# A hybrid retention and attention block on Trainium2: another table of times for side work in the attention, and stores issued by another engine

## The chip, the cores and the metric

The kernel runs on one core of one Trainium2 chip. The metric is the device time of one execution in microseconds; a profile shows one execution, engine by engine. TensorE (PE) multiplies matrices, VectorE (DVE), ScalarE (ACT) and GpSimd (POOL) do elementwise work, and SyncE (SP) issues nearly all DMA transfers. Each engine runs its own list of instructions strictly in order and waits at an instruction until its inputs are there; a DMA transfer is issued by an instruction of some engine's list and then runs on the DMA engines.

## The reference

One layer in fp32, for a sequence of 1024 tokens of width 1024, with 16 learned meta tokens put in front:

```python
u = _rms_norm(h, pre_w)
z = u @ w_in                       # one input projection for all branches
rq, rk, rv, rg, aq, ak, av, ag, gr, ga = _split_in(z)
...                                # bidirectional retention, 4 heads -> o_r, normed, gated by silu(rg)
y_r = o_r.astype(h.dtype) @ w_rb
...
o_a = _windowed_sink_attention(aq, ak, av, sink)[:, META_PAD:].reshape(B, T, ATT_Q)
o_a = o_a * jax.nn.silu(ag.astype(jnp.float32))
y_a = o_a.astype(h.dtype) @ w_ab
mix = jax.nn.sigmoid(gr) * y_r + jax.nn.sigmoid(ga) * y_a
out = mix @ w_o
return h + _rms_norm(out, post_w)
```

The attention has 8 heads of 128 in 2 key groups, a window of 128 positions to either side, the meta tokens always visible, and a sink logit per head; `aq` and `ak` are rotated by position first.

## The kernel before

Every fp32 matrix is split into a high and a low part, and `mm3` (L74 to L76) does three matmuls for one product. The program goes through setup and first projections, the retention heads (to about 335 us), the attention (to about 565 us), and then four phases of large products: gates (z), the retention branch, the attention branch and the output projection. The large products use a scheme with seven block products instead of eight, which needs sums and differences of blocks of the operands. Those of x are made on the side during the attention, and go to DRAM (`xs_d`); some blocks of the gates' product are worked out in the attention too (`pe`), and go to DRAM as `e`.

The attention is 32 chunks (hp, n): a pair of heads hp = 0 to 3, a block of 128 queries n = 0 to 7; the text writes chunk k = 8 hp + n. Chunk k of the loop issues stage 1 of chunk k + 1 (scores `ps` on PE, mask and maximum `raw`, `nm` on VectorE at L1369, exp `p` on ScalarE at L1372, scaling by 1/sum on POOL, in the last two chunks on ScalarE at L1379), stage 2 of chunk k (transposes `pt` on PE, high parts `pah`, `pm`, `pbh` on ScalarE, low parts on VectorE), 5 to 10 steps of filler for PE, and stage 3 of chunk k - 1 (output products `po`, copied by ScalarE to `oa`, L1440, and stored to `oTa_d` after each second chunk, L1443).

A step of filler is one `mm3`: 200 steps in all, of projections of later queries and keys (`paq`, `pak`) and of the partial gate products `pe7` to `pe13`. A projection's result is rotated by `rope_late`: two products on VectorE (`m_aq`, `aq`), and two transfers by POOL that add `m_aq` into `aq` (`akr` and `m_ak` for keys). `split_q` then makes the high and low half of queries (`aqh` by ScalarE at L641, `aql` by VectorE), `keys` those of keys (`kTh` by ScalarE at L687, `kTl` by VectorE).

Side work is hung on the steps by the table `BEGUN`: after step number s, `hooked` issues the functions of entry s. They are
- `sum_fetch`, `sum_row`: load row q of 8 of x (two tiles `xs0q`, `xs1q` of 256 KB each, two buffers), scale it on ScalarE (L726), four differences on VectorE (L729), store it by SP (L732);
- `fetch_aq`, `fetch_ak`, `half_w`: load weights (`wr`, two buffers) and split them (`wh` by ScalarE at L116, `wl` by VectorE). `wr17` holds those of the last queries;
- `pre_fetch`, `pre_sum`, `pre_parts`: load the weights of one partial gate product (`we`, 512 KB each, in the same two buffers), three sums on VectorE (L774), high part `weh` on ScalarE (L784), low part `wel` on VectorE. After the last one the buffers go to the first weights of z (`wrz`).

The scheduler that turns the program into one list for each engine keeps the order of the text where `issue_after` says so; else it moves instructions by its own costs. Three 1 MB pieces of x are copied from DRAM to DRAM into the output by `x_to_out` on SP's queue (the normed result is added to them at the end). The copy waits for nothing; `issue_after` only fixes its place, behind the last store of `oTa`:

```python
            if k in (12, 17, 21):
                x_to_out({12: 0, 17: 4, 21: 6}[k])
```

The stores of `e` (20, L806) and of `oTa` (16, L1443) are issued by SP, in one list with all loads.

Of the kernel before, what the change touches and what calls it, by code (L numbers as in the profile page):

```python
# [16 lines left out]
P = 128  # L17
# [21 lines left out]
def block_kernel(ctx: ExitStack, tc: tile.TileContext, x0, xT, x, meta, w_in, w_rb, w_ab, w_out, post_w,  # L39
                 rope, tab, out):  # L40
    nc = tc.nc
# [17 lines left out]
    oTa_d = dram.tile([KT, P, SEQ], F32, tag="oTa", name="oTa_d")  # L59
# [5 lines left out]
    e_d = {(u, p): dram.tile([P, 512], F32, tag=f"e{u}{p}", name=f"e{u}_{p}") for u in PRE for p in PRE[u]}  # L65
    xs_d = [dram.tile([4, P, 2, 512], F32, tag=f"xs{i}", name=f"xs{i}") for i in range(2)]
# [120 lines left out]
    def rope_evac(t, a, b, o, nm):  # L187
# [13 lines left out]
    neg, na, e, e2, s_, ss, acc, lg = (ra.tile([P, 8], F32, name=n) for n in (  # L201
        "neg", "na", "e", "e2", "s_", "ss", "acc", "lg"))
# [63 lines left out]
    with tc.tile_pool(name="setup", bufs=1, reuse_waits="tile") as st:  # L266
# [57 lines left out]
        for k in range(KT):  # L324
            t = xr[k]
# [395 lines left out]
    def sum_row(q, part):  # L721

        k, c = q // 2, slice(256 * (q % 2), 256 * (q % 2) + 256)
        if not part:
            for i, t in xsum.items():
                nc.scalar.activation(t, t, AF.Copy, scale=vec[:, 4 * i + k:4 * i + k + 1])  # L726
# [31 lines left out]
    def pre_fetch(u):  # L758
        n = P * len(PRE[u])
        raw = [keep.tile([P, 4, 256], F32, tag="wr", bufs=2, name=f"we{u}_{j}") for j in range(len(PRE[u]))]  # L760
        for j, t in enumerate(reversed(raw)):
            nc.sync.dma_start(t[:, :, 0:n], w_in[gates[u], :, 4 - 4 * j:8 - 4 * j, 0:n])
        fetched_w[u] = raw

    def pre_sums(u, only=range(3)):

        raw, n = fetched_w[u], P * len(PRE[u])
        t = raw[-1]
        if n > P:
            v = t[:, :, P:n]  # L770
            for i in only:
                a, b, op = ((raw[0][:, :, P:n], v, ALU.add), (v, raw[0][:, :, 0:P], ALU.subtract),
                            (t[:, :, 0:P], v, ALU.subtract))[i]
                nc.vector.tensor_tensor(v, a, b, op)  # L774
# [4 lines left out]
    def pre_parts(u):  # L779

        t, n = fetched_w.pop(u)[-1], P * len(PRE[u])
        h = wp.tile([P, 4, 256], R, tag="wh", bufs=4, name=f"weh{u}")[:, :, 0:n]
        l = wp.tile([P, 4, 256], R, tag="wl", bufs=4, name=f"wel{u}")[:, :, 0:n]
        nc.scalar.copy(h, t[:, :, 0:n])  # L784
        dve_lo(l, t[:, :, 0:n], h)
        parts[u] = h, l

    def gen_pre(u):

        if u not in parts:  # L790
            if u not in fetched_w:
                pre_fetch(u)
                pre_sums(u)
            pre_parts(u)
        h, l = parts.pop(u)
        for p in PRE[u]:
# [8 lines left out]
            nc.scalar.copy(o, b)  # L805
            nc.sync.dma_start(e_d[u, p], o)  # L806
            yield

    def hooked(gens, at):
# [522 lines left out]
    def attention():  # L1332
        oa = [None]
# [95 lines left out]
        def stage3(hp, n):  # L1429
            g = hp // 2  # L1430
            bl, m = st2.pop((hp, n))
            po = p3(f"po{hp}_{n}")
            for j, (b, h_, l_) in enumerate(bl):
                mm3(po[:, 0:256], *(t[:, P * g:P * g + P] for t in (vah[:, b], low_value(b))), h_, l_, j == 0, False)
            latest[:] = [nc.tensor.matmul(po[:, 0:256], vm[:, P * g:P * g + P], m, start=False,
                                          stop=True).ins]
            if n % 2 == 0:
                oa[0] = ap.tile([P, 2, 256], F32, tag="oa", bufs=2, name=f"oa{hp}_{n}")
            o0 = P * (n % 2)
            last["oa"] = nc.scalar.copy(oa[0][:, :, o0:o0 + P],  # L1440
                                        po[:, 0:256].rearrange("p (e t) -> p e t", e=2)).ins
            if n % 2:
                stored.append(nc.sync.dma_start(  # L1443
                    oTa_d[2 * hp:2 * hp + 2, :, P * (n - 1):P * (n + 1)].rearrange("e p t -> p e t"), oa[0]).ins)

# [12 lines left out]
        for k, (hp, n) in enumerate(chunks):  # L1458
            ends = k >= len(chunks) - 2
            if k + 1 < len(chunks):  # L1460
                with follow(*latest, *marks("oa", "lo")):
                    stage1(*chunks[k + 1])
                if chunks[k + 1] == (1, NB - 1):
                    keys(1, 0)
            if chunks[k] == (3, NB - 2):

                with follow(*latest):
                    fill(FILL[hp][n])
                yield
            if not k:  # L1470
                with follow(*latest):
                    fill(FILL[hp][n] - 3)
            with follow(*latest, *marks("exp", "sum")) if not ends else ExitStack():
                stage2(hp, n)
            if k and not ends:
                with follow(*latest):
                    fill(FILL[hp][n])
            with follow(*latest) if not ends else ExitStack():
                if k:
                    stage3(*chunks[k - 1])  # L1480
            if ends:
                yield
            if k in (12, 17, 21):
                x_to_out({12: 0, 17: 4, 21: 6}[k])
        stage3(*chunks[-1])


# [9 lines left out]
             82: [(split_q, 2, 0, 0)], 88: [(sum_row, 3, 0)], 89: [(sum_row, 3, 1)], 90: [(split_q, 2, 1, 0)],  # L1497
             91: [(sum_fetch, 4)], 96: [(sum_row, 4, 0)], 97: [(sum_row, 4, 1)], 99: [(sum_fetch, 5)],
             104: [(keys, 1, 1)], 105: [(fetch_aq, 3)], 107: [(sum_row, 5, 0)], 108: [(sum_row, 5, 1)],
             110: [(sum_fetch, 6)], 112: [(split_q, 2, 0, 1)], 114: [(half_w, 'q', 3, 0)],  # L1500
             116: [(half_w, 'q', 3, 1)], 118: [(pre_fetch, 9)], 121: [(sum_row, 6, 0)], 122: [(sum_row, 6, 1)],
             123: [(keys, 1, 2)], 124: [(sum_fetch, 7)], 125: [(pre_sum, 9, 0)], 128: [(pre_sum, 9, 1)],
             129: [(split_q, 2, 1, 1)], 130: [(pre_sum, 9, 2)], 133: [(pre_parts, 9)], 134: [(pre_fetch, 10)],
             136: [(keys, 1, 3)], 139: [(sum_row, 7, 0)], 140: [(sum_row, 7, 1)], 145: [(split_q, 3, 0, 0)],
             146: [(pre_sum, 10, 0)], 147: [(pre_sum, 10, 1)], 149: [(pre_sum, 10, 2)], 152: [(split_q, 3, 1, 0)],
             153: [(pre_parts, 10)], 154: [(pre_fetch, 11)], 161: [(pre_sum, 11, 0)], 162: [(pre_sum, 11, 1)],
             163: [(pre_sum, 11, 2)], 164: [(split_q, 3, 0, 1)], 167: [(pre_parts, 11)], 168: [(pre_fetch, 12)],
             169: [(split_q, 3, 1, 1)], 173: [(pre_sum, 12, 0)], 174: [(pre_sum, 12, 1)], 175: [(pre_sum, 12, 2)],
             177: [(pre_parts, 12)], 178: [(pre_fetch, 13)], 182: [(pre_sum, 13, 0)], 183: [(pre_sum, 13, 1)],
             184: [(pre_sum, 13, 2)], 187: [(pre_parts, 13)]}  # L1510

    def x_to_out(r):

        with tc.issue_after(stored[-1]):
            nc.sync.dma_start(out[P * r:P * r + 2 * P], x[P * r:P * r + 2 * P])

    del wak[:]
    i = attention()
    next(i)

# [102 lines left out]
```

## Time and profile before

| | |
|---|---|
| median of 3 runs | 1069.37 us (1068.57 to 1070.4) |
| profiled execution | 1068.98 us |
| its span on the core | 1067.2 us |
| granted TensorE clock over the span | 0.995 |
| busy PE / VectorE / ScalarE / POOL | 1050.3 / 839.7 / 505.8 / 233.0 us |

The span runs from the first to the last instruction of the profile; the profiled execution's own time is 1.8 us longer. A row of the timeline gives start, duration, engine, line and operation, what is written and read, and in brackets how long the engine was idle before it and what ended the wait. SPq and POOLq are the engines' issues of DMA. Windows give, for each stretch, its length and then the busy time of PE, of its weight loads, and of the other engines, the granted clock of TensorE and the mean busy share of the DMA engines. Names in rows of the profile have no buffer numbers: `we` there stands for `we9_1` as well as for `we10_1`.

### The profile page before, as it was taken

What the parts mean: (1) busy time and instruction counts of PE and PEld (TensorE: products, weight loads), DVE (VectorE), ACT (ScalarE), POOL (GpSimd) and SP (SyncE); (2) the same over time, 40 slices, a digit from 0 to 9 for tenths busy, and PEclk for the clock granted to TensorE, in tenths of its full rate; (3) what the DMA queues carried; (4) which work ended last, traced back from release to release, by engine and by line L of the source; (5) the groups of instructions that cost most, each with busy time, mean ns of one, the idle gap of its engine ahead of it and who ended that gap; (6) DMA issues with size and microseconds to landing.
All of it is one profiled execution on the core that took longest, in us unless ns stands there. A gap on an engine that the chain in (4) does not pass through costs nothing.

```text
span 1067.2 us, 17268 instructions
## 1 busy us (share of the span) xinstructions
PE 1050.3 (98%) x5880; PEld 908.4 (85%) x5880; DVE 839.7 (79%) x1788; ACT 505.8 (47%) x1127; POOL 233.0 (22%) x338
## 2 busy tenths in 40 slices
PE   9999999999999999989999999999999999999997
PEld 8998999989999888977888888887888888788886
DVE  7886768758875777767768988998799799778665
ACT  5531422523424566555667544455456546334433
POOL 3345245243342432524310000000000000011032
PEclk9999999999999999989999999999999999999999
DMA  9433222242331465665548769899934756789463
GB/s 351 165 84 85 79 32 80 70 109 75 103 72 50 110 187 159 161 203 143 149 154 285 246 228 332 272 348 353 372 117 158 242 172 227 223 222 321 122 119 79
DMA packets 96760, 188.44 MB, mean 177 GB/s; under 512 B 10945, under 2 KB 35553, under 8 KB 95857
## 3 DMA queue, kind: packets, MB, share of 16 engines
q1 hardware_dynamic: 86352, 172.33, 48.0%
q0 software_dynamic: 10176, 14.73, 9.2%
q8 instruction: 46, 0.75, 0.3%
q10 hardware_dynamic: 144, 0.29, 0.1%
q14 instruction: 42, 0.34, 0.1%
HBM read 124.32 MB, written 57.68 MB: 171 GB/s over the span
## 4 chain that ended last, share of the span: by engine, by line
PE 89%; DMA 5%; DVE 3%; ACT 1%; issue 1%; DVEq 0%; POOLq 0%; POOL 0%; ACTq 0%; SPq 0%
PE bz L75 7%; PE bz L74 7%; PE bz L76 7%; PE pv L76 3%; PE pv L75 3%; PE pv L74 3%; PE ba L75 2%; PE br L74 2%; PE br L75 2%; PE ba L74 2%; PE ba L76 2%; PE br L76 2%; PE bo L75 2%; PE bo L74 2%; PE bo L76 2%; PE paq L75 2%
## 5 line engine op out<-in xcount | busy, mean ns | idle before, releaser
L1246 POOL DMA_DIRECT2D mx_d<-c1a x4 | 3.6, 890 | 402.4 <-DVE c1a L1237 383.2
L75 PE MATMUL bz<-T,llz 128*128 128x512 f32 x192 | 76.2, 397 | 0.0
L74 PE MATMUL bz<-T,lhz 128*128 128x512 f32 x192 | 75.6, 395 | 0.0
L76 PE MATMUL bz<-T,lhz 128*128 128x512 f32 x192 | 75.4, 393 | 0.0
L74 PE MATMUL pv<-wh,big 128*128 128x256 f32 x256 | 73.4, 287 | 0.0
L75 PE MATMUL pv<-wh,big 128*128 128x256 f32 x256 | 73.2, 286 | 0.0
L76 PE MATMUL pv<-wl,big 128*128 128x256 f32 x256 | 73.2, 286 | 0.0
L75 PE MATMUL bz<-big,llz 128*128 128x512 f32 x176 | 69.6, 395 | 0.2 <-DVE llz L90 0.2
L76 PE MATMUL bz<-big,lhz 128*128 128x512 f32 x176 | 69.5, 395 | 0.0
L74 PE MATMUL bz<-big,lhz 128*128 128x512 f32 x176 | 68.8, 395 | 0.2 <-ACT lhz L942 0.2
L1382 POOL TENSOR_SCALAR p<-p,den 128x400 f32<-128x400 f32 (+1 forms) x60 | 40.4, 776 | 80.6 <-DVE den L1375 73.8
L1372 ACT ACTIVATE p<-raw,nm 128x401 f32<-128x401 f32 (+1 forms) x64 | 38.2, 599 | 41.1 <-DVE nm L1369 40.9
L74 PE MATMUL paq<-big,wh 128*128 128x512 f32 x128 | 51.8, 404 | 0.0
L75 PE MATMUL paq<-big,wl 128*128 128x512 f32 x128 | 50.6, 395 | 0.0
L76 PE MATMUL paq<-big,wh 128*128 128x512 f32 x128 | 50.6, 395 | 0.0
L76 PEld LDWEIGHTS pv<-wl,big 128*128 128x128 f32 x256 | 48.3, 189 | 0.4
L74 PEld LDWEIGHTS pv<-wh,big 128*128 128x128 f32 x256 | 48.3, 188 | 0.4
L75 PEld LDWEIGHTS pv<-wh,big 128*128 128x128 f32 x256 | 48.3, 189 | 0.3
L1369 DVE CUSTOM_DVE_ANT_0 raw<-ps,mask,nsink 128x400 f32<-128x400 f32 (+1 forms) x64 | 36.3, 598 | 10.7 <-PE ps L76 10.2
L90 DVE TENSOR_TENSOR wl<-wr,wh 128x1024 fp32r<-128x1024 f32 x28 | 34.9, 1250 | 11.8 <-POOL wh L87 6.8
L74 PEld LDWEIGHTS bz<-T,lhz 128*128 128x128 f32 x192 | 36.0, 188 | 9.1 <-ACT u2z L1024 0.2
L76 PEld LDWEIGHTS bz<-T,lhz 128*128 128x128 f32 x192 | 36.0, 188 | 8.8
(616 smaller groups left out, 3613.1 us busy)
## 6 DMA issues: line engine op xcount, KB each, us to landing
wrz<-in_w_in_dram SPq DMA_DIRECT2D x32, 512.0 KB, 5.7
wr<-in_w_in_dram SPq DMA_DIRECT2D x29, 512.0 KB, 3.7
e<-e SPq DMA_DIRECT2D x40, 256.0 KB, 4.2
we<-in_w_in_dram SPq DMA_DIRECT2D x16, 512.0 KB, 4.3
tg<-tg_d SPq DMA_DIRECT2D x32, 256.0 KB, 4.7
T<-preT SPq DMA_DIRECT2D x6, 1024.0 KB, 7.9
xn<-in_x_dram SPq DMA_DIRECT2D x8, 512.0 KB, 9.2
oTr_d<-ost SPq DMA_DIRECT2D x16, 256.0 KB, 2.1
```

The source lines that it names most:

```text
L74: nc.tensor.matmul(o, ah, bh, start=first, stop=False, **kw)
L75: nc.tensor.matmul(o, al, bh, start=False, stop=False, **kw)
L76: latest[:] = [nc.tensor.matmul(o, ah, bl, start=False, stop=last, **kw).ins]
L90: return nc.vector.tensor_tensor(o, i, hi.bitcast(F32), ALU.subtract).ins
L1246: nc.gpsimd.dma_start(d, to, accum_op=ALU.add)
L1369: nc.vector.tensor_tensor_reduce(raw[e_][:, 1:1 + wid], s[:, 0:wid], mask[:, mo:mo + wid], -SCALE, nsink[:, hd:hd + 1], ALU.add, ALU.min, ...
L1372: last["exp"] = nc.scalar.activation(p[:, 0:1 + wid], raw[e_][:, 0:1 + wid], AF.Exp, scale=-1.0, bias=nm_[:, e_:e_ + 1], accum_out=den[:, ...
L1382: nc.gpsimd.tensor_scalar(pt[e_][:, 0:wid], pt[e_][:, 0:wid], den[:, e_:e_ + 1], 1.0, op0=ALU.mult, op1=ALU.mult)
```

## The change

It does three things. The table `BEGUN` gets other steps. Rows 0 to 7 of x are summed at 34, 48, 61, 75, 88, 100, 123 and 146 (before: 34, 48, 74, 88, 96, 107, 121 and 139) and loaded at 10, 39, 52, 65, 79, 92, 105 and 127 (before: 10, 39, 52, 78, 91, 99, 110 and 124). Loads, first sums and halves of the partial gate products 9 to 13 go to 122, 141, 158, 171, 182 (before 118, 134, 154, 168, 178), to 133, 150, 166, 176, 187 (before 125, 146, 161, 173, 182) and to 140, 157, 170, 181, 190 (before 133, 153, 167, 177, 187). The halves of the last queries' weights go to 117 and 121 (before 114 and 116), keys (1, 2) to 116 (before 123), and some `split_q` and `fetch_aq` move by two to eight steps. Second, the copies of x follow chunks 12, 14 and 21, each behind the latest store of a row of sums. Third, ScalarE issues the stores of `e` and `oTa`. The line numbers of the changed kernel are one lower than before from the table on.

```diff
--- before.py
+++ after.py
@@ -729,7 +729,7 @@
             nc.vector.tensor_tensor(x[o], x[a], x[b], ALU.subtract)
         if part:
             for i, t in xsum.items():
-                nc.sync.dma_start(xs_d[i][k][:, :, c], t)
+                last["xs"] = nc.sync.dma_start(xs_d[i][k][:, :, c], t).ins
 
     xsum = {}
 
@@ -803,7 +803,7 @@
                     yield
             o = ra.tile([P, 512], F32, tag="m", bufs=4, name=f"e{u}_{p}")
             nc.scalar.copy(o, b)
-            nc.sync.dma_start(e_d[u, p], o)
+            nc.scalar.dma_start(e_d[u, p], o)
             yield
 
     def hooked(gens, at):
@@ -827,7 +827,7 @@
             yield from gen_pre(u)
 
     pre, fetched_w, parts = all_pre(), {}, {}
-    softmax, stored, last = [], [], {}
+    softmax, last = [], {}
 
     def marks(*names):
         return [last[m] for m in names if m in last]
@@ -1440,8 +1440,8 @@
             last["oa"] = nc.scalar.copy(oa[0][:, :, o0:o0 + P],
                                         po[:, 0:256].rearrange("p (e t) -> p e t", e=2)).ins
             if n % 2:
-                stored.append(nc.sync.dma_start(
-                    oTa_d[2 * hp:2 * hp + 2, :, P * (n - 1):P * (n + 1)].rearrange("e p t -> p e t"), oa[0]).ins)
+                nc.scalar.dma_start(
+                    oTa_d[2 * hp:2 * hp + 2, :, P * (n - 1):P * (n + 1)].rearrange("e p t -> p e t"), oa[0])
 
 
 
@@ -1480,8 +1480,8 @@
                     stage3(*chunks[k - 1])
             if ends:
                 yield
-            if k in (12, 17, 21):
-                x_to_out({12: 0, 17: 4, 21: 6}[k])
+            if k in (12, 14, 21):
+                x_to_out({12: 0, 14: 4, 21: 6}[k])
         stage3(*chunks[-1])
 
 
@@ -1492,26 +1492,25 @@
...
-             61: [(split_q, 1, 0, 1)], 65: [(split_q, 1, 1, 1)], 68: [(half_w, 'k', 1, 0)],
-             72: [(half_w, 'k', 1, 1)], 74: [(sum_row, 2, 0)], 75: [(sum_row, 2, 1)], 78: [(sum_fetch, 3)],
...
+             61: [(sum_row, 2, 0)], 62: [(sum_row, 2, 1)], 65: [(sum_fetch, 3)], 66: [(split_q, 1, 0, 1)],
...
     def x_to_out(r):
 
-        with tc.issue_after(stored[-1]):
+        with tc.issue_after(last["xs"]):
             nc.sync.dma_start(out[P * r:P * r + 2 * P], x[P * r:P * r + 2 * P])
 
     del wak[:]
```

The first place is ScalarE's list around the key cast `kTh1_2` (hp 2, chunks 17 and 18; in the names, `p2_2` is the exp of chunk (2, 2), `wh17_0` and `wh17_1` are the halves of the last queries' weights, `xs06` and `xs16` the tiles of row 6). Before:

```order
L116 CAST wh17_0_6420<-wr17_0_6266 128x1024
L116 CAST wh17_1_6430<-wr17_1_6267 128x1024
L1440 COPY oa1_6_6380<-po1_7_6457 128x2x128
L1372 ACTIVATE p2_2_6469,den2_2_6468<-raw4_6293,nm2_2_6467 128x401
L1372 ACTIVATE p2_2_6469,den2_2_6468<-raw5_6301,nm2_2_6467 128x401
L1410 CAST pah2_1_6496<-pt1_2_1_6487 128x512
L1413 CAST pm1_4889<-pt2_2_1_6492 32x128 x2
L1420 CAST pbh2_1_6501<-pt2_2_1_6492 128x256
L726 ACTIVATE xs06_6345<-xs06_6345,vec_101 128x512
L726 ACTIVATE xs16_6347<-xs16_6347,vec_101 128x512
L687 CAST kTh1_6206<-akr1_2_6352 128x256
```

Now:

```order
L116 CAST wh17_0_6432<-wr17_0_6256 128x1024
L687 CAST kTh1_6206<-akr1_2_6357 128x256
L1440 COPY oa1_6_6381<-po1_7_6452 128x2x128
L1443 DMA oTa_d_67<-oa1_6_6381 128x2x256
L1372 ACTIVATE p2_2_6464,den2_2_6463<-raw4_6306,nm2_2_6462 128x401
L1372 ACTIVATE p2_2_6464,den2_2_6463<-raw5_6314,nm2_2_6462 128x401
L1410 CAST pah2_1_6491<-pt1_2_1_6482 128x512
L1413 CAST pm1_4889<-pt2_2_1_6487 32x128 x2
L1420 CAST pbh2_1_6496<-pt2_2_1_6487 128x256
L116 CAST wh17_1_6506<-wr17_1_6257 128x1024
```

The key cast stands ahead of the exp instead of behind it, one half of `wh17` has moved behind the next exp, row 6 comes later, and the store of `oa1_6` is an instruction of this list.

The second place is SP's list around the second copy of x (`xs0_91` and `xs1_92` are the DRAM tensors of sums, `out_0_dram` the output). Before:

```order
L762 DMA we9_1_6441<-in_w_in_dram 128x1024
L1443 DMA oTa_d_67<-oa1_6_6380 128x2x256
L1515 DMA out_0_dram<-in_x_dram 16x16384
L762 DMA we9_0_6440<-in_w_in_dram 128x1024
L732 DMA xs0_91<-xs06_6345 256x1x256
L732 DMA xs1_92<-xs16_6347 256x1x256
L719 DMA xs07_6530<-in_xT_dram 128x2x256
L719 DMA xs17_6532<-in_xT_dram 128x2x256
```

Now:

```order
L732 DMA xs0_91<-xs05_6086 256x1x256
L732 DMA xs1_92<-xs15_6088 256x1x256
L1514 DMA out_0_dram<-in_x_dram 16x16384
L719 DMA xs06_6278<-in_xT_dram 128x2x256
L719 DMA xs16_6280<-in_xT_dram 128x2x256
L762 DMA we9_1_6514<-in_w_in_dram 128x1024
L762 DMA we9_0_6513<-in_w_in_dram 128x1024
L732 DMA xs0_91<-xs06_6278 256x1x256
L732 DMA xs1_92<-xs16_6280 256x1x256
```

The copy stands behind the two stores of row 5 and ahead of the loads of row 6, the two loads of `we9` come after it and with nothing between them, and the store of `oa1_6` is gone from the list.

The third place is the end of the attention, where ScalarE's list has the high part of the last partial gate product, `weh13`. Before:

```order
L1420 CAST pbh3_5_7482<-pt2_3_5_7473 128x256
L784 CAST weh13_7495<-we13_1_7343 128x1024
L805 COPY e12_2_7492<-pe12_2_7424 128x512
L1379 ACTIVATE p3_6_7450<-p3_6_7450,den3_6_7449 128x400 x2
L805 COPY e12_3_7512<-pe12_3_7499 128x512
L1440 COPY oa3_4_7526<-po3_4_7515 128x2x128
L1388 COPY pm2_3_6_7466<-p3_6_7450 128x64
```

Now:

```order
L1420 CAST pbh3_5_7479<-pt2_3_5_7470 128x256
L805 COPY e12_2_7489<-pe12_2_7422 128x512
L1379 ACTIVATE p3_6_7447<-p3_6_7447,den3_6_7446 128x400 x2
L806 DMA e12_2_87<-e12_2_7489 128x512
L805 COPY e12_3_7512<-pe12_3_7493 128x512
L1388 COPY pm2_3_6_7463<-p3_6_7447 128x64
L806 DMA e12_3_88<-e12_3_7512 128x512
L1440 COPY oa3_4_7526<-po3_4_7515 128x2x128
L784 CAST weh13_7505<-we13_1_7413 128x1024
```

`weh13` has gone from the first of these to the last, behind the copies of `e12`, the scalings of `p3_6` and two stores.

PE's list at its use: before, `pe13` begins ahead of the transposes of chunk (3, 6):

```order
L76 MATMUL ps7_7_7537<-kTl1_6207,aqh3_11_7191 128x272
L74 MATMUL pe13_2_7548<-big1_0_110,weh13_7495 128x512
L74 MATMUL pe13_3_7564<-big1_0_110,weh13_7495 128x512
L1399 MATMUL pt1_3_6_7625<-ident_118,p3_6_7450 128x128
L1404 MATMUL pt2_3_6_7630<-ident_118,p3_6_7450 128x128
L75 MATMUL pe13_2_7548<-big1_0_110,wel13_7496 128x512
L76 MATMUL pe13_2_7548<-big1_1_112,weh13_7495 128x512
```

Now:

```order
L76 MATMUL po3_5_7646<-pbl3_5_7480,vah_533 128x256
L1435 MATMUL po3_5_7646<-pm1_4889,vm_534 128x256
L74 MATMUL pe13_2_7548<-big1_0_110,weh13_7505 128x512
L74 MATMUL pe13_3_7564<-big1_0_110,weh13_7505 128x512
L75 MATMUL pe13_2_7548<-big1_0_110,wel13_7506 128x512
L76 MATMUL pe13_2_7548<-big1_1_112,weh13_7505 128x512
L74 MATMUL pe13_2_7548<-big1_0_110,weh13_7505 128x512
```

It begins behind those transposes and behind the output products of chunk (3, 5).

More of the change, by code (lines that the diff above doesn't have):

```diff
@@ L1499, in block_kernel @@
[L1499 to L1508, printed above, removed]
@@ L1509, in block_kernel @@
-             177: [(pre_parts, 12)], 178: [(pre_fetch, 13)], 182: [(pre_sum, 13, 0)], 183: [(pre_sum, 13, 1)],
-             184: [(pre_sum, 13, 2)], 187: [(pre_parts, 13)]}
+             61: [(sum_row, 2, 0)], 62: [(sum_row, 2, 1)], 65: [(sum_fetch, 3)], 66: [(split_q, 1, 0, 1)],
+             68: [(half_w, 'k', 1, 0)], 72: [(half_w, 'k', 1, 1)], 73: [(split_q, 1, 1, 1)], 75: [(sum_row, 3, 0)],
+             76: [(sum_row, 3, 1)], 79: [(sum_fetch, 4)], 82: [(split_q, 2, 0, 0)], 88: [(sum_row, 4, 0)],
@@ new lines, in block_kernel @@
+             89: [(sum_row, 4, 1)], 90: [(split_q, 2, 1, 0)], 92: [(sum_fetch, 5)], 100: [(sum_row, 5, 0)],
+             101: [(sum_row, 5, 1)], 102: [(fetch_aq, 3)], 104: [(keys, 1, 1)], 105: [(sum_fetch, 6)],
+             110: [(split_q, 2, 0, 1)], 116: [(keys, 1, 2)], 117: [(half_w, 'q', 3, 0)], 121: [(half_w, 'q', 3, 1)],
+             122: [(pre_fetch, 9)], 123: [(sum_row, 6, 0)], 124: [(sum_row, 6, 1)], 127: [(sum_fetch, 7)],
+             129: [(split_q, 2, 1, 1)], 133: [(pre_sum, 9, 0)], 134: [(pre_sum, 9, 1)], 136: [(keys, 1, 3)],
@@ new lines, in block_kernel @@
+             139: [(pre_sum, 9, 2)], 140: [(pre_parts, 9)], 141: [(pre_fetch, 10)], 145: [(split_q, 3, 0, 0)],
+             146: [(sum_row, 7, 0)], 147: [(sum_row, 7, 1)], 150: [(pre_sum, 10, 0)], 152: [(pre_sum, 10, 1)],
+             153: [(split_q, 3, 1, 0)], 154: [(pre_sum, 10, 2)], 157: [(pre_parts, 10)], 158: [(pre_fetch, 11)],
+             164: [(split_q, 3, 0, 1)], 166: [(pre_sum, 11, 0)], 167: [(pre_sum, 11, 1)], 168: [(pre_sum, 11, 2)],
+             170: [(pre_parts, 11)], 171: [(pre_fetch, 12)], 172: [(split_q, 3, 1, 1)], 176: [(pre_sum, 12, 0)],
@@ L1512, in x_to_out @@
+             178: [(pre_sum, 12, 1)], 179: [(pre_sum, 12, 2)], 181: [(pre_parts, 12)], 182: [(pre_fetch, 13)],
+             187: [(pre_sum, 13, 0)], 188: [(pre_sum, 13, 1)], 189: [(pre_sum, 13, 2)], 190: [(pre_parts, 13)]}
     def x_to_out(r):
-        with tc.issue_after(stored[-1]):
+        with tc.issue_after(last["xs"]):
             nc.sync.dma_start(out[P * r:P * r + 2 * P], x[P * r:P * r + 2 * P])
```

2 lines of the change are left out of this document (removed).

## The prediction

> **What bounds the kernel now.** I read the page first (who is busy, and in which slices not), then the table of windows over the gap that it shows, then PE's waits there, and then what ScalarE, VectorE and the queues did in front of that wait.
>
> ```profile
> span 1067.2 us, 17268 instructions
> PE 1050.3 (98%) x5880; PEld 908.4 (85%) x5880; DVE 839.7 (79%) x1788; ACT 505.8 (47%) x1127; POOL 233.0 (22%) x338
> PE   9999999999999999989999999999999999999997
> PEclk9999999999999999989999999999999999999999
> ```
>
> TensorE is the bound: it is idle for 16.9 us of the whole span. Apart from the tail (the 7 at the end), slice 18 alone (453 to 480 us) falls short, in busy time and in clock. By windows (PE's column comes first; PEclk and the DMA share stand behind the engines):
>
> ```profile
> 460.00:480.00 20.00, 14.96 (x88) 13.59 (x87) 13.32 (x33) 10.17 (x27) 5.27 (x10) 0.83 0.74 226
> 480.00:500.00 20.00, 17.95 (x101) 15.13 (x100) 15.94 (x39) 10.71 (x29) 9.82 (x15) 1.00 0.48 115
> ...
> 470.00:472.00 2.00, 1.05 (x3) 1.04 (x4) 1.86 (x6) 1.17 (x3) 0.02 (x1) 0.50 0.63 212
> 472.00:474.00 2.00, 2.00 (x9) 1.88 (x9) 0.42 (x1) 0.00 (x0) 0.00 (x0) 0.50 0.73 206
> 474.00:476.00 2.00, 2.00 (x11) 1.82 (x10) 0.00 (x0) 0.00 (x0) 0.00 (x0) 0.67 0.97 335
> ```
>
> From 460 to 500 us PE idles 5.04 + 2.05 = 7.1 us. Behind the long gap its clock is 0.50 to 0.67, which costs 1.05 x 0.50 + 2.00 x 0.50 + 2.00 x 0.33 = 2.2 us more. These 9.3 us are the prize; the other 9.8 us of idle time lie outside these 40 us. The waits in this stretch:
>
> ```profile
> PE ps L74 <- ACT kTh L687: 5.0, 1, 5.0
> PE ps L75 <- DVE aql L90: 1.3, 1, 1.3
> PE ps L76 <- DVE kTl L90: 0.4, 1, 0.4
> ```
>
> The scores of chunk (2, 3) wait 5.0 us for the keys kTh1_2. What held ScalarE, and the queues beside it (SP's copy of x at L1515; POOL's transfer of m_aq into aq by L185; rows with DMA behind the time are pieces of the chain; in the last five the number at the end is the median from issue to landing, first of the stretch 463 to 476, then, in the last two, of the whole run):
>
> ```profile
> 454.12 0.62 ACT L641 CAST aqh<-aq 128x512 fp32r<-128x512 f32 x1 [1.83 <-DMA aq<-m_aq]
> 457.38 0.72 ACT L726 ACTIVATE xs<-xs,vec 128x512 f32<-128x512 f32 x1 [2.64 <-DMA xs<-in_xT_dram]
> 461.32 2.00 ACT L116 CAST wh<-wr 128x1024 fp32r<-128x1024 f32 x2
> 469.27 1.33 ACT L726 ACTIVATE xs<-xs,vec 128x512 f32<-128x512 f32 x2
> 470.51 0.39 ACT L687 CAST kTh<-akr 128x256 fp32r<-128x256 f32 x1
> ...
> 461.80 0.82 PE L1399 MATMUL pt<-ident,p 128*128 128x128 f32 x4
> 476.46 0.69 DVE L774 TENSOR_TENSOR we<-we,we 128x512 f32<-128x512 f32 x1 [4.04 <-DMA we<-in_w_in_dram]
> 482.03 0.68 DVE L90 TENSOR_TENSOR aql<-aq,aqh 128x512 fp32r<-128x512 f32 x1
> ...
> 465.99 0.61 SPq L1515 DMA_DIRECT2D out_dram<-in_x_dram  x1
> 438.08 6.08 DMA xs<-in_xT_dram
> 454.56 2.71 DMA xs<-in_xT_dram
> 466.71 9.66 DMA we<-in_w_in_dram
> ...
> we<-in_w_in_dram SPq DMA_DIRECT2D x2, 512.0 KB, 7.4
> aq<-m_aq POOLq DMA_DIRECT2D x2, 128.0 KB, 9.3
> out_dram<-in_x_dram SPq DMA_DIRECT2D x1, 8.7
> ...
> aq<-m_aq POOLq DMA_DIRECT2D x32, 128.0 KB, 3.3
> we<-in_w_in_dram SPq DMA_DIRECT2D x16, 512.0 KB, 4.3
> ```
>
> ScalarE goes through its list in order. It idles 2.64 us for a load of row 5 of the sums, which shifts all behind it (exp, both halves of wh17, 2.00 us); then exp p2_2 must come before the casts of row 6 (1.33 us), and only behind those, at 470.51, kTh1_2. The second stall hangs on the load of we9, issued behind the 1 MB copy of x: 9.66 us. VectorE sits 4.04 us in the first sum of we9, with the masks of the scores queued behind it; aql2_11, late with its rotated queries (9.3 us to landing), comes at 482.03, and PE has waited 1.3 us for it.
>
> **The change part by part.** *Table of rows.* Rows 5 and 6 move from steps 107 and 121 to 100 and 123, and their casts no longer stand between this exp and this key cast. The 2.64 us were the end of a longer string: the store of row 3 was behind the first copy of x, so the load of row 4 took 6.08 us, its sum and store were late, and the load of row 5 was issued only at 454.56. Now a copy is issued behind both stores of a row; the loads of row 5 are issued near 438 and 440, land with the first copy at the latest (438 + 6.1 = 444), and are cast near 447. Rows 6 and 7 are fetched 18 and 19 steps ahead of their sums, against 11 and 15. So this wait goes. One half of wh17 instead of two stands ahead of kTh1_2, and the exp of p2_2 now comes behind it. Worked with the durations above: aqh2_10 ends at 454.74, the exps of p2_1 follow their scores at 456, the cast of half wh17 ends by about 460, and kTh1_2 by 461 (0.39 us). PE's last work ahead of the wait ended at 465.9 (kTh1_2 was done at 470.9, less the 5.0). That leaves 5 us of slack: the 5.04 us go, and with them the 2.2 us of clock.
>
> *we9 and the copy.* The pieces 0, 4 and 6 of x go to DRAM behind the chunks 12, 14 and 21. No copy is then ahead of we9: issued near 467 when wl17_1 frees its buffer, it lands at the median of its kind, 4.3 us, near 472, and its first sum stands 8 steps later than before, at 133 (near 475 without the stall). So the 4.04 us of VectorE go; with its queries not behind a copy, aql2_11 stands ahead of the first we9 sum and is on time. The 1.3 us and what else is in the 2.05 us go too, except for the 0.4 us at kTl, which I keep as a loss: kTl1_3 still stands behind a we9 sum. Gain of the two parts: 9.3 - 0.4 = 8.9 us.
>
> *Stores on ScalarE's queue.* 16 of oTa, 20 of e.
>
> ```profile
> L1443 SPq DMA_DIRECT2D oTa_d<-oa x16: 367/382/879, 362.6 to 577.2; - x16
> L806 SPq DMA_DIRECT2D e<-e x20: 319/326/559, 94.6 to 563.4; - x20
> L288 ACTq DMA_DIRECT2D head<-in_x_dram x1: 402/402/402, 0.7 to 0.7; - x1
> SPq L806 <- ACT e L805: 55.6, 13, 9.7
> ```
>
> The only issue on ScalarE's queue cost 402 ns, SP's 326 to 382 ns. I take 0.40: 36 x 0.40 = 14.4 us of ScalarE, at most one store or three per chunk. ScalarE is busy for 47%, and between its copy of oa and the next exp it waits anyway (0.94 us in the row at 550.77 below), which covers the one oTa store per two chunks. Cover gone, the bound is 14.4 us; I take nothing. On the other side SP no longer stands 55.6 us in waits for e, but what it issues behind them had leads of chunks, so I take no gain either.
>
> *End of attention.* The halves of the partial gate products are made later: the lead of pre_parts ahead of its first use falls from 27, 15, 9, 7 and 5 steps to 20, 11, 6, 3 and 2. The rows there now:
>
> ```profile
> 550.77 0.63 ACT L1372 ACTIVATE p<-raw,nm 128x401 f32<-128x401 f32 x1 [0.94 <-DVE nm L1369]
> 553.30 1.05 ACT L784 CAST weh<-we 128x1024 fp32r<-128x1024 f32 x1
> 557.00 0.52 ACT L1372 ACTIVATE p<-raw,nm 128x273 f32<-128x273 f32 x1 [0.22 <-DVE nm L1369]
> 554.38 1.23 DVE L90 TENSOR_TENSOR wel<-we,weh 128x1024 fp32r<-128x1024 f32 x1
> 556.57 0.64 PE L74 MATMUL pe<-big,weh 128*128 128x512 f32 x2
> 564.66 0.50 PE L75 MATMUL bz<-big,llz 128*128 128x512 f32 x1 [0.15 <-DVE llz L90]
> 555.64 0.33 SPq L1177 DMA_DIRECT2D wrz<-in_w_in_dram  x1
> ```
>
> weh13 stood ahead of the copies of e12, the two scalings of p3_6, pm and oa; all of these ended by 556.8 (557.00 less 0.22). Put behind them, and with two stores (0.8 us) among them, weh13 ends at 557.6 to 557.9 instead of 554.35, and wel13 (1.23) at 559.1 at the latest. PE meets pe13 at 556.57 plus the transposes and the output products that it now does first (about 1.95 us), 558.5; its second product needs wel13 by 559.0. A stall of 0.3 us. wrz0_1, which takes over that buffer, is issued 3.5 us later; the first low half of z then arrives some 0.4 us late, beside 0.15 before. Bounds of the two: nothing, and 3.5 us if the whole delay reaches PE. I take 0.6, since the orders leave PE other work for most of it.
>
> **Sum.** -9.3 + 0.4 + 0.6 = -8.3 us. The profiled execution took 1068.98 us (span 1067.2), which gives 1060.7; the median of the three runs is 0.4 above it, so 1061.1. I forecast **1061**. From no change at all, a measurement of this kernel can tell about 0.2%, 2.1 us.
>
> **Rivals.** *The copy moves the stall.* Behind chunk 14 it is issued near 451.5, between the transfers of aq2_10 and of akr1_2 as they lay before. Before, aq<-m_aq landed 9.3 us after its issue beside a copy, and 3.3 us otherwise. If it is held to the copy's end, 451.5 + 8.7 = 460.2, ScalarE casts aqh2_10 there instead of at 454.12, the exps of p2_1 end near 462, and PE, which takes p2_1 at 461.8, waits 1 to 3 us; with the end of attention at its bound, 3.5, the loss is 1 to 5 us: 1062 to 1066. The Trainium skill, "DMA: Bandwidth & Descriptors", section "Queues, rings and completion order", says that each DMA engine takes turns between the queues at the grain of packets; by that a small transfer from POOL's queue would need about twice its 3.3 us beside the copy, 6.6 us as an estimate, and this stall would not exist. The trace does not bear that out here: 9.3 us, longer than the copy itself. The Trainium skill, "TensorE: Matmul & The Clock Gate", Part 1, puts the fall of the clock at an idle stretch of about 3.4 us; by it only the upper end of this rival would pay in clock too, an estimate of 2.2 us as behind the 5.0 us gap above.
>
> *The stall stays.* The same bytes are moved in the same stage, and the DMA engines are at 0.74 from 460 to 480. If it is this load and not the place of the copy that makes we9 and the rotated rows late, the waits of 4.04 and 2.64 us come back at another load, and the time is 1067.5 to 1070. Against it: the next 20 us have a share of 0.48, so there is room to move into.
>
> *Slower: ScalarE stands in a store.* A store issued in order also waits for an older transfer, whose counter it uses again; the program has such a wait at 14 of the 36. On SP such waits held loads with long leads; on ScalarE the exp of the next chunk stands behind. If each of the stores in attention that has one (12) meets a transfer of 6 to 10 us in flight, like those beside the copies above, and is held 2 us beyond its 0.94 us of cover, that is 12 x 1 to 2 = 12 to 24 us, less 8.3: 1073 to 1085. It decides from 8.3 us of such holds on. Against it: the transfers waited for are eight issues older, and at the median even the 512 KB of a we need 4.3 us.
>
> **How the numbers follow.** Forecast (1059 to 1062.5) 0.60; the copy moves the stall, 0.20; the stall stays, 0.08; slower, 0.12. The low end is 1069.4 - 9.3 - 0.9 (how far the runs lie apart below the median) = 1059, the high end the second case's with 0.5 to spare, 1066.5; together they hold 0.80. Faster by over 0.2% is below 1067.2: 0.80. Same 0.08. Slower 0.12.
>
> **What would show it.** Right: PE at 19.9 or more of 20 us and a clock of 1.00 from 460 to 480; no wait of ps for kTh over 0.5 us; the we9 load at 4 to 5 us; copies of x near 437, 451 and 490 us; ScalarE's issues at 0.4 us, with no wait of its queue over 1 us; between 556 and 567 PE idle under 1.2 us. Wrong: a wait of pt or ps for p or aq between 455 and 465, of pe for wel over 1 us, or waits of ScalarE's queue for DMA.

## The result, and the profile after

The changed kernel takes 1060.63 us (median of 6 runs, 1059.47 to 1061.79), the kernel before 1069.88 us (6 runs beside these, 1067.88 to 1072.45). The ratio is 0.9915, with a 95% interval of 0.9901 to 0.9929: 9.1 us less, 7.6 to 10.6. The forecast was 1061.

The page of the changed kernel, the four rows that were shown of the kernel before:

```profile
span 1057.9 us, 17223 instructions
PE 1046.8 (99%) x5880; PEld 906.2 (86%) x5880; DVE 838.6 (79%) x1788; ACT 506.8 (48%) x1127; POOL 230.6 (22%) x338
PE   9999999999999999999999999999999999999997
PEclk9999999999999999999999999999999999999999
```

The span is 9.3 us shorter (1067.2 before). PE's idle time is 1057.9 - 1046.8 = 11.1 us, against 16.9, and its busy time, for the same 5880 matmuls, 3.5 us less. Slice 18 no longer stands out in either row. Windows and PE's waits of the changed kernel in the attention (the waits from 455 to 565 us):

```profile
460.00:480.00 20.00, 19.65 (x123) 17.53 (x123) 16.94 (x43) 12.41 (x34) 8.76 (x14) 1.00 0.59 152
480.00:500.00 20.00, 20.00 (x114) 17.48 (x113) 15.18 (x40) 11.89 (x32) 6.53 (x12) 1.00 0.66 169
500.00:540.00 40.00, 39.46 (x230) 34.73 (x229) 29.42 (x71) 23.95 (x64) 12.97 (x24) 1.00 0.50 149
540.00:560.00 20.00, 19.75 (x115) 17.07 (x114) 13.75 (x31) 14.31 (x38) 0.00 (x0) 1.00 0.70 231
...
PE ps L75 <- DVE aql L90: 0.6, 2, 0.3
PE bz L75 <- DVE llz L90: 0.3, 1, 0.3
PE pt L1399 <- POOL p L1382: 0.2, 1, 0.2
```

From 460 to 500 us 0.35 us of idle time is left of 7.1, at a clock of 1.00; the wait for kTh1_2 is gone from the list. From 500 to 560 some 0.8 us have come in small waits. What ScalarE does at that place now, the transfers around it (the last number of the two rows without a start is the median time from issue to landing, of those issued from 447 to 458 us), and the first sum of we9:

```profile
459.78 0.41 ACT L687 CAST kTh<-akr 128x256 fp32r<-128x256 f32 x1 [1.57 <-DMA akr<-m_ak]
462.59 0.64 ACT L1372 ACTIVATE p<-raw,nm 128x401 f32<-128x401 f32 x1 [2.01 <-DVE nm L1369]
...
450.15 1.08 SPq L1514 DMA_DIRECT2D out_dram<-in_x_dram  x1
akr<-m_ak POOLq DMA_DIRECT2D x2, 64.0 KB, 7.3
out_dram<-in_x_dram SPq DMA_DIRECT2D x1, 8.0
...
477.27 0.68 DVE L774 TENSOR_TENSOR we<-we,we 128x512 f32<-128x512 f32 x1
```

ScalarE still waits, 1.57 us for the rotated keys, which the second copy of x holds up (7.3 us to landing, beside a copy of 8.0); but the cast then ends at 460.2, ahead of the exp of chunk (2, 2) and 4.4 us ahead of the scores of chunk (2, 3), which start at 464.64. The first sum of we9 starts behind other work of VectorE at 477.27, with no wait for its load.

### The profile page after: what moved, and what is told of

It is laid out like the page before. It is cut to its first block, busy times and chain, and to the rows that moved or that the text cites. A ratio compares the mean times of both kernels' runs of the same rounds, so it can differ in the third digit from the quotient of the medians.

```text
span 1057.9 us, 17223 instructions
## 1 busy us (share of the span) xinstructions
PE 1046.8 (99%) x5880; PEld 906.2 (86%) x5880; DVE 838.6 (79%) x1788; ACT 506.8 (48%) x1127; POOL 230.6 (22%) x338
## 4 chain that ended last, share of the span: by engine, by line
PE 90%; DVE 4%; DMA 4%; ACT 1%; issue 1%; POOL 0%; SPq 0%; DVEq 0%; POOLq 0%; ACTq 0%
PE bz L75 6%; PE bz L76 6%; PE bz L74 6%; PE pv L75 3%; PE pv L74 3%; PE pv L76 3%; PE paq L75 3%; PE paq L76 3%; PE paq L74 3%; PE ba L75 2%; PE br L75 2%; PE br L74 2%; PE ba L74 2%; PE br L76 2%; PE ba L76 2%; PE bo L75 2%
## 5 line engine op out<-in xcount | busy, mean ns | idle before, releaser
L76 PEld LDWEIGHTS bz<-T,lhz 128*128 128x128 f32 x192 | 36.0, 188 | 8.9
L75 PEld LDWEIGHTS bz<-T,llz 128*128 128x128 f32 x192 | 36.0, 188 | 8.7 <-DVE llz L90 0.2
```

The lines of the kernel that those rows point to most:

```text
L75: nc.tensor.matmul(o, al, bh, start=False, stop=False, **kw)
L76: latest[:] = [nc.tensor.matmul(o, ah, bl, start=False, stop=last, **kw).ins]
```

## The experiments

First the parts: the table and the copies of x each alone, the change without its stores, and the stores alone; then the entries of the table one by one. Differences of time in this section come from the ratio to runs of the kernel before on the same chip, taken of its 1069 us.

**The table alone**: the whole of `BEGUN` as in the change, in the kernel before. Two of its pieces:

```diff
-             61: [(split_q, 1, 0, 1)], 65: [(split_q, 1, 1, 1)], 68: [(half_w, 'k', 1, 0)],
...
-             123: [(keys, 1, 2)], 124: [(sum_fetch, 7)], 125: [(pre_sum, 9, 0)], 128: [(pre_sum, 9, 1)],
+             61: [(sum_row, 2, 0)], 62: [(sum_row, 2, 1)], 65: [(sum_fetch, 3)], 66: [(split_q, 1, 0, 1)],
...
+             110: [(split_q, 2, 0, 1)], 116: [(keys, 1, 2)], 117: [(half_w, 'q', 3, 0)], 121: [(half_w, 'q', 3, 1)],
```

> The kernel before with the new table alone: copies of x still behind chunks 12, 17 and 21, all stores on SP. Theory (the place of the key cast in ScalarE's list, and the spacing of the rows of sums, made the long stall): the wait of ps for kTh1_2 falls from 5.0 us to under 0.5 us, the clock stays at 1.00, but the load of we9 is still issued behind a copy and takes 8 to 10 us, so 1 to 2 us of waits stay at aql or kTl; about 7 us less than before, 1061 to 1064 us. Rival (the copies of x alone made both stalls): the stalls stay at some other load or rotated row, 1067 to 1070 us.

Measured: 1063.12 us, ratio 0.9947 (0.9933 to 0.9961), 5.7 us less, inside the theory's range. PE's longest wait after the start, what VectorE and SP did ahead of it, and the windows around it:

```profile
PE ps L75 <- DVE aql L90: 1.3, 1, 1.3
...
487.47 0.74 SPq L1514 DMA_DIRECT2D out_dram<-in_x_dram  x1
495.90 0.69 DVE L774 TENSOR_TENSOR we<-we,we 128x512 f32<-128x512 f32 x1 [1.91 <-DMA we<-in_w_in_dram]
501.70 0.85 DVE L90 TENSOR_TENSOR aql<-aq,aqh 128x512 fp32r<-128x512 f32 x1
...
500.00:502.00 2.00, 1.27 (x11) 1.04 (x9) 1.97 (x7) 0.78 (x2) 2.00 (x4) 1.00 0.50 74
502.00:504.00 2.00, 1.16 (x6) 0.92 (x7) 1.99 (x6) 0.32 (x1) 1.66 (x2) 0.91 0.94 147
504.00:506.00 2.00, 2.00 (x8) 1.58 (x7) 0.86 (x2) 1.95 (x8) 0.76 (x2) 0.50 0.84 302
506.00:508.00 2.00, 2.00 (x8) 1.64 (x7) 0.74 (x3) 0.78 (x1) 0.45 (x2) 0.74 0.00 2
```

Both old stalls are gone with the copies at their old chunks. What is left is of the kind expected, 20 us later: the copy behind chunk 21, at 487.5 here, holds up the load of `we` issued behind it (7.5 us to landing); VectorE sits 1.91 us in the first sum of it, and from there on hardly pauses until the low part of a half of queries, at 501.70, for which PE waits 1.3 us. The copy holds up one of the two transfers of these queries too (7.7 us), but they were there by 496, and their high part was cast at 499.78 without a wait. The clock falls behind the wait (0.91, 0.50 and 0.74), which makes the price 1.6 us of idle time and another 1.6 of clock in this execution.

**The copies alone**, in the kernel before:

```diff
-                nc.sync.dma_start(xs_d[i][k][:, :, c], t)
+                last["xs"] = nc.sync.dma_start(xs_d[i][k][:, :, c], t).ins
...
-            if k in (12, 17, 21):
-                x_to_out({12: 0, 17: 4, 21: 6}[k])
+            if k in (12, 14, 21):
+                x_to_out({12: 0, 14: 4, 21: 6}[k])
...
-        with tc.issue_after(stored[-1]):
+        with tc.issue_after(last["xs"]):
```

> The kernel before with the copies of x alone moved (behind chunks 12, 14 and 21, each behind the latest store of a row of sums); table and stores as before. Theory (order of the casts and spacing of the rows): row 5's load now lies behind the second copy, ScalarE waits for it 2 to 5 us, and the wait for kTh1_2 stays at 4 to 7 us; only the second stall (about 2 us, we9) goes: 1066 to 1070 us. Rival (the copies alone made both stalls): both go, 1060 to 1063 us.

Measured: 1067.47 us, ratio 0.9991 (0.9983 to 1.0): 1.0 us less, hardly clear of nothing.

```profile
PE ps L74 <- ACT kTh L687: 3.2, 1, 3.2
PE ps L76 <- DVE kTl L90: 2.6, 1, 2.6
```

The stall stays, as the theory had it, but split over the high and the low half of the same keys: 3.2 us for the first, where 4 to 7 had been expected. So the place of the copies alone did not make it.

**The change with its stores back on SP**:

```diff
-            nc.scalar.dma_start(e_d[u, p], o)
+            nc.sync.dma_start(e_d[u, p], o)
...
-                nc.scalar.dma_start(
+                nc.sync.dma_start(
```

> The changed kernel with the stores of e and oTa back on SP: table and copies as changed. Theory (the stores were worth nothing): within 1.5 us of the changed kernel, 1059.5 to 1062.5 us. Rival (the longer leads of the loads only work with SP free of these waits): a load of we or of a row is issued 3 to 10 us later, and 2 to 6 us of waits come back, 1063 to 1067 us.

Measured: 1060.72 us, ratio 0.9923 (0.9911 to 0.9936): the changed kernel's time. In this order of work the stores are worth nothing that can be measured; table and copies together give 8.2 us (6.8 to 9.5) of the 9.1 (7.6 to 10.6).

**The stores alone**, in the kernel before:

```diff
-            nc.sync.dma_start(e_d[u, p], o)
+            nc.scalar.dma_start(e_d[u, p], o)
...
-                stored.append(nc.sync.dma_start(
+                stored.append(nc.scalar.dma_start(
```

> The kernel before with only the stores of e and oTa issued by ScalarE. Theory (hidden work on both engines): within 1.5 us of the kernel before, the same three waits of PE within 0.5 us each, ScalarE's issues 0.33 to 0.40 us. Rival (SP's waits for these stores held loads that PE needed): 2 to 4 us less. Third (ScalarE is late for an exp or a cast because of the stores): 1 to 5 us more.

Measured: 1073.64 us, ratio 1.0047 (1.0034 to 1.0061): 5.0 us slower. The size is that of the third theory, the reason is not: it is no store that makes ScalarE late.

```profile
PE pv L161 <- ACT wh L116: 3.6, 1, 3.6
PE ps L74 <- ACT kTh L687: 3.0, 1, 3.0
...
L1515 SPq DMA_DIRECT2D out_dram<-in_x_dram x3: 510/527/668, 13.4 to 17.3; - x3
```

The wait that is new is at 30 us, in the setup: the three copies are issued at 13.4 to 17.3 us, among the loads of weights (`wr`), and ScalarE waits for one of these. They are placed by `issue_after` behind a store that is now in ScalarE's list, and nothing holds them in SP's own list any more. The change, which moves the stores too, anchors them at `last["xs"]`, an instruction of SP. The run shows one thing more: with no copy anywhere in the attention the wait for kTh1_2 is still 3.0 us.

**The stores alone, the copies held**: as above, and the copies placed behind a load of `we` or a store of a row, so that SP's list keeps its order around them:

```diff
+                last["xs", i] = nc.sync.dma_start(xs_d[i][k][:, :, c], t).ins
...
+            last["we", j] = nc.sync.dma_start(t[:, :, 0:n], w_in[gates[u], :, 4 - 4 * j:8 - 4 * j, 0:n]).ins
...
-        with tc.issue_after(stored[-1]):
+        with tc.issue_after(last["we", 0] if r == 4 else last["xs", 0]):
```

> The kernel before with the stores of e and oTa issued by ScalarE, and the copies of x held at their places in SP's list by instructions of SP's own list (in the run with the stores alone they had gone to the setup, since what they were placed behind was no longer in SP's list). Theory (the stores are worth nothing, the 5 us of that run came from the copies in the setup): 1067 to 1071 us, the wait for kTh1_2 4 to 6 us. Rival (ScalarE's issues make casts late): 1071.5 to 1075 us, with a wait for kTh1_2 of 6 us or more, or new waits on ScalarE.

Measured: 1067.24 us, ratio 0.9983 (0.9974 to 0.9992): 1.8 us less, inside the range given.

```profile
PE ps L74 <- ACT kTh L687: 5.0, 1, 5.0
PE ps L75 <- DVE aql L90: 0.2, 1, 0.2
```

The 5.0 us stay as they were; the second wait falls from 1.3 to 0.2 us. So the 5 us lost in the run before were the copies in the setup, and ScalarE's issues cost nothing that shows. Whether the 1.8 us come from the stores is not shown: the new anchors also put the second copy 2.0 us earlier (463.98 instead of 465.99), and VectorE's wait for the load of we9, which sets the second wait, is 2.63 us instead of 4.04. The three parts alone give 5.7 + 1.0 + 1.8 = 8.5 us, all together 9.1.

**What in the table does it.** One entry: the key cast. First forward in the kernel before, from 123 to 116:

```diff
-             116: [(half_w, 'q', 3, 1)], 118: [(pre_fetch, 9)], 121: [(sum_row, 6, 0)], 122: [(sum_row, 6, 1)],
-             123: [(keys, 1, 2)], 124: [(sum_fetch, 7)], 125: [(pre_sum, 9, 0)], 128: [(pre_sum, 9, 1)],
+             116: [(keys, 1, 2), (half_w, 'q', 3, 1)], 118: [(pre_fetch, 9)], 121: [(sum_row, 6, 0)], 122: [(sum_row, 6, 1)],
+             124: [(sum_fetch, 7)], 125: [(pre_sum, 9, 0)], 128: [(pre_sum, 9, 1)],
```

> The kernel before with one entry of the table moved: the keys (1, 2) at step 116 instead of 123. Copies, stores and rows of sums as before. Theory (the long stall is the place of the key cast behind the exp and the casts of row 6): the wait for kTh1_2 falls from 5.0 us to under 0.5 us and its cost in clock goes, while the load of we9 behind the second copy still costs 1.5 to 4 us: 1061 to 1065 us. Rival (the rows of sums and the copies make ScalarE late, whatever the cast's place): a wait of 3 us or more stays at another input of the scores or transposes of chunks 17 to 19: 1066 to 1070 us.

Measured: 1067.8 us, ratio 0.9984 (0.9973 to 0.9995), 1.7 us less: the rival's case in time, though its wait is not in one piece. Rows of PE's waits:

```profile
PE pt L1399 <- DVE pal L90: 1.8, 3, 1.4
PE ps L74 <- DVE nm L1369: 1.1, 1, 1.1
PE ps L75 <- DVE aql L90: 0.8, 1, 0.8
PE ps L76 <- DVE kTl L90: 0.5, 1, 0.5
```

No row for kTh is left, but the waits have moved to the next things, 4.2 us in these four rows: the maxima and low parts of the same chunks. ScalarE still waits for the row's load (3.4 us here), and both halves of wh17 and wl17 are still packed into one chunk.

Then back in the changed kernel, from 116 to 125:

```diff
-             110: [(split_q, 2, 0, 1)], 116: [(keys, 1, 2)], 117: [(half_w, 'q', 3, 0)], 121: [(half_w, 'q', 3, 1)],
-             122: [(pre_fetch, 9)], 123: [(sum_row, 6, 0)], 124: [(sum_row, 6, 1)], 127: [(sum_fetch, 7)],
+             110: [(split_q, 2, 0, 1)], 117: [(half_w, 'q', 3, 0)], 121: [(half_w, 'q', 3, 1)],
+             122: [(pre_fetch, 9)], 123: [(sum_row, 6, 0)], 124: [(sum_row, 6, 1)], 125: [(keys, 1, 2)], 127: [(sum_fetch, 7)],
```

> The changed kernel with one entry of the table moved: the keys (1, 2) at step 125, behind the row 6 sum at 123 and 124, as the order was before. Theory (place of the cast): the scores of chunk (2, 3) wait 1 to 2.5 us for kTh1_2 or kTl1_2, and the clock may fall for some 3 us behind that: 1061.5 to 1065 us. Rival (the spacing of rows and the copies alone removed the stall): no wait over 0.5 us, within 1 us of the changed kernel.

Measured: 1061.5 us, ratio 0.9933 (0.9921 to 0.9946); the theory's wait is there:

```profile
PE ps L74 <- ACT kTh L687: 2.1, 1, 2.1
```

In the changed kernel the place of the cast is worth those 2 us, and in the time about 1 to 2 (0.9 by the medians, 1.9 by the ratios).

**Rows of sums against the rest of the table** (in the kernel before: the entries of `sum_fetch` and `sum_row` at their steps of the new table and all others at their old ones; then the reverse). The steps of the rows, summed up (not lines of the edit):

```text
before  sum_fetch 3..7: 78, 91, 99, 110, 124   sum_row 2..7, first half: 74, 88, 96, 107, 121, 139
now     sum_fetch 3..7: 65, 79, 92, 105, 127   sum_row 2..7, first half: 61, 75, 88, 100, 123, 146
```

> The kernel before with only the entries of the rows of sums (sum_fetch, sum_row) from the new table; weights, keys, queries, partial gate products, copies and stores as before. Theory (several pieces of side work crowd ScalarE and VectorE between chunks 16 and 18, and each part of the table removes a share): ScalarE's wait for a row's load (2.64 us) is gone, but kTh1_2 still stands behind both halves of wh17 and the exp of chunk (2, 2); wait for it 1 to 3 us, and the load of we9 behind the copy costs 1 to 2 us: 1062 to 1066 us. Rival (the rows' loads were the whole cause): no wait for kTh1_2 over 0.5 us, 1060 to 1062.5 us.

Measured: 1066.36 us, ratio 0.997 (0.996 to 0.9981), 3.2 us less, a little above the theory's range.

```profile
PE ps L75 <- DVE aql L90: 3.7, 1, 3.7
PE ps L74 <- ACT kTh L687: 0.7, 1, 0.7
...
465.63 0.41 ACT L687 CAST kTh<-akr 128x256 fp32r<-128x256 f32 x1
465.93 1.34 ACT L726 ACTIVATE xs<-xs,vec 128x512 f32<-128x512 f32 x2
```

> The kernel before with all entries of the new table but those of the rows of sums: keys (1, 2) earlier, the two halves of wh17 four steps apart, partial gate products later. Theory (crowding): no wait for kTh1_2 over 0.5 us, but the wait of ScalarE for the row's load stays (2.5 to 3.5 us) and makes exps or low parts late; waits of PE of 1 to 3 us in sum between 455 and 490: 1062 to 1066 us. Rival (the weights' halves and the key were the whole cause): under 0.8 us of waits there, 1060 to 1062.5 us.

Measured: 1064.0 us, ratio 0.9954 (0.9939 to 0.9969), 4.9 us less, inside the theory's range.

```profile
PE pt L1399 <- DVE pal L90: 1.6, 2, 1.4
PE ps L75 <- DVE aql L90: 1.3, 1, 1.3
```

Neither is the whole. With the rows alone the long wait falls from 5.0 to 0.7 us (1 to 3 had been expected), though the cast still stands behind both halves of wh17 and the exp. But this run moves the cast in one respect too: keys (1, 2) and row 6 now share step 123, and the cast stands ahead of row 6's casts, as the rows show. The second stall, behind the copy and the load of we9, grows from 1.3 to 3.7 us. With the rest alone the key is on time, but ScalarE waits 3.3 us for the row's load (3.28 at 457.52), VectorE idles behind it, and in the chunk after it a low part of the transposes is late.

**The copies on ScalarE's queue**, in the changed kernel:

```diff
-        with tc.issue_after(last["xs"]):
-            nc.sync.dma_start(out[P * r:P * r + 2 * P], x[P * r:P * r + 2 * P])
+        with tc.issue_after(last["oa"]):
+            nc.scalar.dma_start(out[P * r:P * r + 2 * P], x[P * r:P * r + 2 * P])
```

> The changed kernel with the three copies of x issued by ScalarE, near the same times. Theory (a copy holds every other transfer in flight, whatever queue it is on): loads of rows by SP and transfers of akr1_2 by POOL issued while the copy runs land with its end or later, 5 to 8 us after issue; time within 1.5 us of the changed kernel. Rival (queues take turns by packet, as the Trainium skill, DMA: Bandwidth & Descriptors, section Queues, rings and completion order, says): those transfers land in 3 to 5 us beside the copy, and the copy takes 9 us or more.

Measured: 1059.8 us, ratio 0.9915 (0.9902 to 0.9929), the changed kernel's time. The second copy goes out at 447.7 us here, 2.4 us earlier. Transfers issued from 447.4 to 456 us, with the median of their times to landing:

```profile
xs<-xs SPq DMA_DIRECT2D x2, 256.0 KB, 8.6
aq<-m_aq POOLq DMA_DIRECT2D x2, 128.0 KB, 7.8
akr<-m_ak POOLq DMA_DIRECT2D x2, 64.0 KB, 5.6
out_dram<-in_x_dram ACTq DMA_DIRECT2D x1, 6.9
```

With the copy on a third queue SP's store takes 8.6 us and POOL's 128 KB 7.8 us, longer than the copy itself; the rival's 3 to 5 us, beside a copy of 9 or more, did not come. In this order the queries of chunk (2, 4) were the ones held, and that too cost PE nothing.

## Why the prediction was right

*The prize.* All of it came back: 7.1 us of idle time went to 0.35 in the same 40 us, with the clock at 1.00. Against the forecast of -6.1 us for idle time (7.1 less 0.4 and 0.6), it fell by 16.9 - 11.1 = 5.8 us. The term that was too small is the clock's: 2.2 us from three windows, where PE's busy time fell by 3.5. The clock of the whole window from 460 to 480 gives 0.17 x 14.96 = 2.5. From 460 us to one and the same place behind the attention (582.3 before, 573.0 now) PE is busy 115.05 us before and 111.85 now, 3.2 less; where the 0.7 us between these two come from stays open. The 1.3 us more from busy time and the 0.3 us less from idle time are the 1 us by which the span fell further (9.3) than the sum (8.3).

*The step that was right as a sum but not as a cause.* The working named two things for the long stall, the 2.64 us for a row's load and the place of the key cast, behind the casts of row 6 (1.33 us) among others, and took both from one ScalarE list. The new steps of the rows alone take 4.3 of the 5.0 us off this wait, and they undo both: 2.64 + 1.33 is 4.0. The key cast's earlier step alone takes all 5.0 off this wait but only 1.7 us off the time, because the same late chunk then waits for its maxima and low parts. The kernel was late as a chunk, not at one cast. Had the change been the cast alone, this working would have forecast some 7 us (5.0 and 2.2) and missed by 5.

*Late keys.* kTh1_2 was forecast done at 461, and ended at 460.2, though ScalarE waited 1.57 us for it, which the working did not have. What stood ahead of it was done earlier than the working put it, and the slack of 4.4 us (5 forecast) would have covered the rest.

*The copies.* The first rival's mechanism is real (7.3 us for akr1_2 beside the copy), but it took the keys, which had 4.4 us to spare, and not the queries of chunk (2, 4) (aq2_10 in the prediction), which were issued 2 to 3 us ahead of the copy and landed in 4.3. The estimate that the prediction drew from the Trainium skill, "DMA: Bandwidth & Descriptors", section "Queues, rings and completion order", by which an engine takes turns between the queues at the grain of packets, was 6.6 us for such a transfer beside a copy. Beside the third copy of the changed kernel the queries took just that:

```profile
aq<-m_aq POOLq DMA_DIRECT2D x2, 128.0 KB, 6.6
out_dram<-in_x_dram SPq DMA_DIRECT2D x1, 6.6
```

Elsewhere they did not: half as many bytes took 7.3 us beside the second copy, and 128 KB took 7.8 with the copy on ScalarE's queue and 9.3 in the kernel before. So twice the usual time does not forecast these transfers; whether the queues take turns by packets no run here shows. The second rival, that the waits come back at another place, is what half the change does (the copies alone 1.0 us, the rows alone a second stall of 3.7).

Two of the signs that the prediction named did not come in: PE is busy 19.65 of the 20 us from 460 to 480, not 19.9, and the third copy is issued at 498.0 us, not near 490.

*The stores.* Taken at nothing, they are nothing (1060.72 against 1060.63). Their issue on ScalarE is 0.33 and 0.38 us at the median, 0.43 at most:

```profile
L806 ACTq DMA_DIRECT2D e<-e x20: 326/326/366, 94.1 to 555.4; - x20
L1443 ACTq DMA_DIRECT2D oTa_d<-oa x16: 366/377/425, 362.0 to 561.3; - x16
```

The rival that ScalarE would stand in a store for an older transfer did not come about at any of the 36.

*End of attention.* Forecast 0.6 us, and the rows at the place:

```profile
544.25 0.64 ACT L1379 ACTIVATE p<-p,den 128x400 f32<-128x400 f32 x1
544.39 0.33 ACTq L806 DMA_DIRECT2D e<-e  x1
544.78 0.63 ACT L1379 ACTIVATE p<-p,den 128x400 f32<-128x400 f32 x1
547.01 1.05 ACT L784 CAST weh<-we 128x1024 fp32r<-128x1024 f32 x1
548.09 1.23 DVE L90 TENSOR_TENSOR wel<-we,weh 128x1024 fp32r<-128x1024 f32 x1 [0.26 <-ACT weh L784]
557.00 0.51 PE L75 MATMUL bz<-big,llz 128*128 128x512 f32 x1 [0.25 <-DVE llz L90]
```

weh13 and wel13 came in time for PE (no wait for either); the low half of z's first weights came 0.25 us late, against 0.15 before. So 0.1 of the 0.6 us came, and of the 0.4 given up at kTl nothing: it has no row any more. But 0.35 us of idle time is left from 460 to 480 us, and 0.54 came from 500 to 504, places that the sum did not name. That the losses still add up to the 1.0 us of the forecast is luck. The 0.3 us that are missing to 5.8 lie in the phase of z, where PE waits 0.5 us for a high part of its weights, against 0.2 before.

## What to carry to other kernels

A stall that shows at one input of the bound engine can be a chunk of work that is late as a whole: moving that input forward then hands the wait to the next one (1.7 us won of 9), while spreading what crowds the chunk (loads, splits, a bulk copy) won all of it here. Place bulk transfers where what is issued beside them has slack: look for what is issued within their length, whatever queue it is on. And an order held by "behind this instruction" holds only in that instruction's list: whoever moves a store to another engine's queue has to look where the things went that were placed behind it.

## What the runs showed of the hardware that was not expected

- An issue of DMA on ScalarE's queue need not take ScalarE's time: the store at 544.39 lies inside an operation that runs from 544.25 to 544.89, and the next one starts at 544.78. The two together take 1.16 us, from 544.25 to 545.41, as with the stores on SP (543.62, 1.16 us in that run). The bound of 14.4 us in the prediction was far too high.
- The granted clock fell to 0.50 behind 1.57 us of idle time within 4 us (0.73 and 0.84 us in the windows from 500 to 504 us of the table alone; the longest single wait there is 1.33). The kernel before has about the same idle time at another place (0.86 and 0.76 us), and its clock stays at 1.00:

```profile
480.00:482.00 2.00, 1.14 (x6) 0.54 (x4) 1.83 (x5) 1.23 (x4) 2.00 (x4) 1.00 0.81 181
482.00:484.00 2.00, 1.24 (x10) 1.20 (x11) 2.00 (x4) 0.00 (x0) 1.64 (x2) 1.00 0.40 85
```

  So a wait of about 1.5 us can cost twice itself, or not; when it does, the runs do not show. Executions of one kernel differ in clock too: with the key cast back at 125 the two longest of five (1062.75 and 1063.26 us) have a granted clock of 0.997 over the span, the three shortest (1060.56 to 1061.5) 0.998 or 0.999, and the profile shown of it is of the longest. The Trainium skill, "TensorE: Matmul & The Clock Gate", Part 1, gives an idle window of about 3.4 us for a fall; the run with the table alone had less than half of that.
- In these traces a transfer issued while a 1 MB copy from DRAM to DRAM runs lands with the copy's end or up to some 4 us behind it, whatever queue it is on, also with the copy on ScalarE's queue and the transfer on another (7.8 us for 128 KB that takes 4.0 at the median of that run).
